# The first mixer's projections in another order: two heads' queries and keys first, the retention inputs late

## The chip, the core and the metric

The kernel runs on one core of a Trainium2 chip. The metric is device time in microseconds for one execution of the whole program, lower is better. TensorE (PE) multiplies matrices into PSUM banks; VectorE (DVE), ScalarE (ACT) and GpSimd (POOL) do the elementwise work; SyncE (SP) issues most of the loads.

## The reference

A batch of 512 tokens by 1024 features goes through two blocks of two layers each. The first block is the one that the change touches (twice, once for each layer):

```python
for l in range(2):
    h = rms_norm(x, norm_mix_pre[l])
    q_da, k_da, v_da, q_r, k_r, v_r, g_r, u_pool = split(h @ w_in[l])   # 512 512 512 128 128 256 256 256 wide
    o_da = diff_attention(q_da, k_da, v_da, ...)   # 4 heads, rotary on q and k, two causal softmaxes each,
                                                   # a0 - lam * a1, times v, rms norm over the head
    o_ret = retention(q_r, k_r, v_r, g_r, ...)     # 4 heads, chunks of 128 tokens with a carried state,
                                                   # group norm, times silu(g)
    o_pool = pool_mixer(u_pool, ...)               # causal means over 2, 4, 8, 16 tokens, minus u, times pool_w
    x = x + rms_norm(concatenate([o_da, o_ret, o_pool]) @ w_out[l], norm_mix_post[l])
    x = x + rms_norm(conv_mlp(rms_norm(x, norm_mlp_pre[l])), norm_mlp_post[l])
```

The second block (feed-forward, another mixer, feed-forward) is not touched.

## The kernel before

The program is a row of ten stages: mix1 and mlp1 for each of the two layers, then ffn1, mix2 and ffn2 twice. All of them share one stream of weights. A chunk is 128 x 1024 numbers; SP loads it (`wraw`, three buffers), ACT rounds it to `whi` (L63) and DVE forms the rest `wlo` (L64), into four pairs of buffers. A chunk's pair is given back by `release`, and the call that gives it back also emits the ACT and DVE instructions that split the chunk four places later. Every dense product is made of three matmuls (hi x hi, hi x lo, lo x hi), so one chunk is 24 matmuls of 512 columns.

There are two ways of multiplying. `fm` makes features by tokens: one chunk, one PSUM bank, and then an evacuation; `fm(..., halves=True)` takes four chunks with four banks and goes through them twice, first for tokens 0 to 255, then for 256 to 511, in 24 matmuls of 256 columns each. `tm` makes tokens by features: four banks at once, one for each tile t of 128 tokens, and its three matmuls for one k go t = 0, 1, 2, 3; with `tail=n` the last n chunks go tile by tile, so that the banks finish one after another.

PSUM has eight banks: four of tag a and four of tag b. In a mixer stage one tag is for the dense products, the other for attention, retention and pooling. These three are written as generators: `diff_attention` (scores, weigh, turn, values, norm, store for 16 pairs of head and tile), `retention` and `pooling`. After each dense triple `tick` adds 640 ns to a clock of credit and steps `bg` and `side` until the credit is used up; what a generator yields is its price. This sets where their instructions stand on every engine; each engine then goes through its own instructions strictly in order. Names in what follows: `psc` scores, `e` their exponentials, `pat` their transposes, `po` values, `on` the normed values, `pot` their transposes (the last step of a head); `pkt`, `prs`, `pst`, `pr`, `rc`, `rsq`, `rn`, `prt` are retention in its order; `pl` and `ppy` are pooling. `mix` holds the eight input tiles of the output product.

Before the change the mixer's order is: `vg` (the retention's values and gate; token-major, tail=4, each token's transposes `ph` just ahead of its products), `v`, q0, k0, qr, kr (the retention's queries and keys), q1, k1, q2, k2, q3, k3, u1, u0 (pooling), and then the output product, whose rows of `w_out` are stored in MIX_ORDER, so that retention and pooling tiles come in at k = 0, 1, 5, 6 and head 3 at k = 7. Queries and keys are evacuated by `rope` (L496): `sh` on DVE (L499), `raw` on DVE (L500), a product on POOL (L501) and a sum on POOL (L502); then, on a later tick, a split on ACT and DVE into `fmq0h` and `fmq0l`. A PSUM bank `pa` is free when `sh` and `raw` have read it. In `fm` without halves these two are emitted ahead of the release of the chunk, with halves behind it.

Of the kernel before, what the change touches and what calls it, by code (L numbers as in the profile page):

```python
# [18 lines left out]
L = 2  # L19
D = 1024  # L20
# [13 lines left out]
MIX_ORDER = (4, 5, 0, 1, 2, 6, 7, 3)  # L34
# [57 lines left out]
class Block:  # L92
# [185 lines left out]
    def tm(self, nk, width, rows, evac, tag, tail=0, opens=False):  # L278
# [24 lines left out]
        for t in range(NT):  # L303
            if opens:
                self.flush(max(self.opened, t))
# [81 lines left out]
    def begin(self, gain):  # L387
# [25 lines left out]
        def turn(t):  # L413
            self.to_h(t, rows.pop(t), "b")
            if t == 1:
                self.st.n_split, self.opened = n_split, 1
# [4 lines left out]
        self.opened = 0  # L421
        self.later(math.inf, 0, lambda: turn(0))
# [103 lines left out]
    def mix1(self, l, next_gain, final):  # L526
# [4 lines left out]
        load = nc.sync.dma_start  # L531
# [12 lines left out]
        load(cols, a["mix_cols"][l])  # L544
        pw = ph.tile([128, 2, 128], F32, name="pw")
        rope_q, rope_k = [], []

        def late_loads():
            load = nc.gpsimd.dma_start
            self.load_masks(3)  # L550
# [27 lines left out]
        def to_fm(name, mask, tab):  # L578
            def evac(ps):
                fm[name] = new_fm(name)  # L580
                self.rope(fm[name], ps, mask, *tab)
            return evac
# [16 lines left out]
        def to_u(c):  # L599
            def evac(ps):  # L600
                self.until(lambda: ("scored", 1) in mix)
# [4 lines left out]
        def to_tm(dst):  # L606
            def evac(t, ps):
                nc.scalar.activation(dst[:, t], ps, AF.Copy)
            return evac

        h_rows = lambda k, t: [x[:, k, t * 128:(t + 1) * 128] for x in self.H]
        free = {"q2": ("scored", 0), "k2": ("scored", 0), "q3": "ret", "k3": ("scored", 1)}
# [3 lines left out]
        def to_vg(t, ps):  # L616
            nc.scalar.activation(vg[:, t, :256], ps[:, :256], AF.Copy)
            nc.scalar.activation(vg[:, t, 256:], ps[:, 256:], AF.Silu)

        self.tm(KD, 512, h_rows, to_vg, dense, tail=4, opens=True)  # L620
        late_loads()
        lambdas()
        self.tm(KD, 512, h_rows, to_tm(v_da), dense, tail=1)
        self.fm([da("q0"), da("k0")])
        self.bg.work.append(self.diff_attention(fm, v_da, neglam, cols[:, 0:1], mix))
        self.fm([to_fm("qr", self.ROPE32, rope_q), to_fm("kr", self.ROPE32, rope_k)])
        self.side.work.append(self.retention(fm, vg, cols[:, 2:4], mix))
        self.fm([da("q1"), da("k1")])
        self.fm([da("q2"), da("k2")])
        self.fm([da("q3"), da("k3")])  # L630
        self.fm([to_u(1), to_u(0)])
        self.side.work.append(self.pooling(u, share, pw, cols[:, 4:6], mix))

        def rows(k, t):
            k = MIX_ORDER[k]
# [8 lines left out]
    def diff_attention(self, fm, v, neglam, gcol, mix):  # L644
# [79 lines left out]
        for i in range(len(units) + 5):  # L724
# [5 lines left out]
            if 1 <= i <= len(units):  # L730
                weigh(*units[i - 1])
                yield 850
            if 2 <= i < len(units) + 2:
                turn(*units[i - 2])
                yield 850
            if 3 <= i < len(units) + 3:
                values(*units[i - 3])
                yield 850
# [12 lines left out]
    def retention(self, fm, vg, gcols, mix):  # L751
# [5 lines left out]
        yield 4000  # L757
# [8 lines left out]
        for h in range(4):  # L766
# [8 lines left out]
            yield 1500  # L775
        state = []
# [14 lines left out]
        for j in range(2):  # L791
# [15 lines left out]
            nc.gpsimd.tensor_mul(s, x, x)  # L807
            nc.vector.reduce_sum(st[:, 2], s, axis=AX)
# [6 lines left out]
            if j == 1:  # L815
                mix["ret"] = True
            yield 2500
# [446 lines left out]
def arrange(inp):  # L1264
# [65 lines left out]
```

## Time and profile before

| | us |
|---|---|
| median of 3 runs | 3435.41 (3434.85 to 3436.55) |
| the profiled execution, its own time | 3436.64 |
| its span in the profile | 3434.9 |
| first mixer stage, until the first product of the MLP | 0 to 243.4 |
| second mixer stage, from its first product to that of the MLP | 613.9 to 843.4 |
| mean granted clock of PE | 0.992 |

The profiled execution's time is 1.7 us above its span; the prediction adds its changes to that time. The first mixer stage also holds the program's opening (the loads of x and the norm of the first rows).

### The profile page before, as it was taken

How to read it: one execution, taken by the hardware profiler on the slowest of the kernel's cores; microseconds unless marked ns; L12 is line 12 of the kernel's file. 1: busy time of each engine (PE TensorE's matmuls, PEld its weight loads, DVE VectorE, ACT ScalarE, POOL GpSimd, SP SyncE). 2: the span in 40 equal slices, each digit the busy share in tenths (PEclk: the TensorE clock that was granted, in tenths of full speed). 3: DMA queues.
4: the chain of work that ended last, by engine and by line, in shares of the span. 5: the costliest groups of instructions: out<-in, count | busy, mean ns of one | idle time of the engine just before them, and what ended most of it. 6: DMA issues, size and time to landing. Idle time of an engine off the chain costs nothing.

```text
span 3434.9 us, 39516 instructions
## 1 busy us (share of the span) xinstructions
PE 3352.0 (98%) x16080; PEld 2770.5 (81%) x16080; DVE 1542.0 (45%) x2013; ACT 1192.8 (35%) x1886; POOL 356.3 (10%) x412
## 2 busy tenths in 40 slices
PE   8999999999999999999999999999999999999999
PEld 6778888767888888888688888888888878888887
DVE  4665542466555243323564533324332457453332
ACT  4344432434443232223533332223222443432222
POOL 2421110242110000000220100000000022010000
PEclk9999999999999999999999999999999999999999
DMA  4122332312233222232112232322232212223232
GB/s 158 49 75 86 104 112 92 108 50 75 86 105 111 92 93 96 95 104 97 59 64 77 90 103 95 104 92 97 95 104 98 96 51 68 82 91 103 94 103 80
DMA packets 87190, 311.99 MB, mean 91 GB/s; under 512 B 10368, under 2 KB 11072, under 8 KB 87008
## 3 DMA queue, kind: packets, MB, share of 16 engines
q1 hardware_dynamic: 85536, 305.17, 26.6%
q0 software_dynamic: 1472, 4.30, 0.4%
q8 instruction: 127, 2.08, 0.2%
q14 instruction: 55, 0.45, 0.0%
HBM read 307.32 MB, written 2.10 MB: 90 GB/s over the span
## 4 chain that ended last, share of the span: by engine, by line
PE 87%; DVE 6%; ACT 3%; POOL 2%; issue 2%; DMA 1%; DVEq 0%; POOLq 0%; ACTq 0%; SPq 0%
PE pa L177 17%; PE pa L178 17%; PE pa L179 17%; PE pb L183 10%; PE pb L184 10%; PE pb L185 10%; DVE wlo L64 1%; PE pz L1121 1%; PE ph L220 1%; PE pos L1121 1%; DVE xn L210 1%; PE pst L986 1%; DVE sh L499 1%; ACT whi L63 0%; PE psc L662 0%
## 5 line engine op out<-in xcount | busy, mean ns | idle before, releaser
L64 DVE TENSOR_TENSOR wlo<-wraw,whi 128x1024 fp32r<-128x1024 f32 x556 | 710.5, 1279 | 1113.1 <-ACT whi L63 1112.0
L177 PE MATMUL pa<-h_hi,whi 128*128 128x512 f32 (+1 forms) x3072 | 1164.5, 379 | 2.0 <-ACT h_hi L162 2.0
L178 PE MATMUL pa<-h_lo,whi 128*128 128x512 f32 (+1 forms) x3072 | 1145.3, 373 | 2.7 <-DVE h_lo L163 2.7
L179 PE MATMUL pa<-h_hi,wlo 128*128 128x512 f32 (+1 forms) x3072 | 1144.5, 373 | 0.0
L63 ACT ACTIVATE whi<-wraw 128x1024 fp32r<-128x1024 f32 x556 | 585.2, 1053 | 635.7 <-PE pb L185 540.7
L177 PEld LDWEIGHTS pa<-h_hi,whi 128*128 128x128 f32 x3072 | 580.5, 189 | 107.6 <-issue 4.9
L179 PEld LDWEIGHTS pa<-h_hi,wlo 128*128 128x128 f32 x3072 | 580.1, 189 | 101.3
L178 PEld LDWEIGHTS pa<-h_lo,whi 128*128 128x128 f32 x3072 | 581.0, 189 | 99.3 <-DVE h_lo L163 4.3
L183 PE MATMUL pb<-whi,hid_hi 128*128 128x512 f32 x1056 | 411.8, 390 | 0.0
L184 PE MATMUL pb<-wlo,hid_hi 128*128 128x512 f32 x1056 | 410.9, 389 | 0.0
L185 PE MATMUL pb<-whi,hid_lo 128*128 128x512 f32 x1056 | 410.9, 389 | 0.0
L183 PEld LDWEIGHTS pb<-whi,hid_hi 128*128 128x128 f32 x1056 | 198.2, 188 | 41.2
L185 PEld LDWEIGHTS pb<-whi,hid_lo 128*128 128x128 f32 x1056 | 198.2, 188 | 41.1
L184 PEld LDWEIGHTS pb<-wlo,hid_hi 128*128 128x128 f32 x1056 | 198.2, 188 | 40.7
L438 ACT ACTIVATE hid_hi<-act 128x512 fp32r<-128x512 f32 x88 | 55.6, 632 | 383.9 <-DVE act L449 383.9
L201 POOL TENSOR_TENSOR rs<-ss 128x1 f32<-128x1 f32 x44 | 12.0, 273 | 1601.8 <-ACT sqs L191 1601.8
L449 DVE TENSOR_TENSOR act<-act,pa 128x512 f32<-128x512 f32 x88 | 60.5, 687 | 210.3 <-PE pa L179 210.3
L458 DVE SCALAR_TENSOR_TENSOR cv<-pa,cw,cv 128x511 f32<-128x511 f32 (+1 forms) x176 | 131.5, 747 | 15.9 <-ACT cv L456 12.8
L445 ACT ACTIVATE act<-pa 128x512 f32<-128x512 f32 x88 | 52.5, 597 | 246.6 <-PE pa L179 246.6
L183 PE MATMUL pb<-whi,h_hi 128*128 128x512 f32 x256 | 108.0, 422 | 11.4 <-DVE fmraw L500 6.7
L184 PE MATMUL pb<-wlo,h_hi 128*128 128x512 f32 x256 | 102.9, 402 | 1.2 <-DVE wlo L64 1.2
L185 PE MATMUL pb<-whi,h_lo 128*128 128x512 f32 x256 | 102.7, 401 | 0.0
(323 smaller groups left out, 2934.5 us busy)
## 6 DMA issues: line engine op xcount, KB each, us to landing
wraw<-w_ffn SPq DMA_DIRECT2D x264, 512.0 KB, 3.2
wraw<-w_mix SPq DMA_DIRECT2D x160, 512.0 KB, 3.3
wraw<-w_mlp SPq DMA_DIRECT2D x132, 512.0 KB, 3.3
X<-x SPq DMA_DIRECT2D x4, 512.0 KB, 7.6
gain<-norm_ffn SPq DMA_DIRECT2D x4, 512.0 KB, 5.3
out<-xn SPq DMA_DIRECT2D x8, 256.0 KB, 2.0
gain<-norm_mix_pre SPq DMA_DIRECT2D x2, 512.0 KB, 5.5
rope_da<-c_rope SPq DMA_DIRECT2D x2, 512.0 KB, 8.4
```

What stands on the lines that cost most here:

```text
L63: self.nc.scalar.activation(hi, t, AF.Copy)
L64: self.nc.vector.tensor_sub(lo, t, hi.bitcast(F32))
L177: mm(ps, w[0], h[0], start=first, stop=False)
L178: mm(ps, w[0], h[1], start=False, stop=False)
L179: mm(ps, w[1], h[0], start=False, stop=last)
L183: mm(ps, h[0], w[0], start=first, stop=False)
L184: mm(ps, h[0], w[1], start=False, stop=False)
L185: mm(ps, h[1], w[0], start=False, stop=last)
L438: nc.scalar.activation(hid[0][:, f], h, AF.Copy)
L449: nc.vector.tensor_mul(g, g, ps)
L458: nc.vector.scalar_tensor_tensor(c[:, s:], ps[:, :T - s], cw[:, j, i:i + 1], c[:, s:], op0=OP.mult, op1=OP.add)
L1121: mm = lambda out, lhsT, rhs, first: nc.tensor.matmul(out, lhsT, rhs, start=first, stop=True, skip_group_check=True)
```

## The change

The projections of the first mixer go in another order: q0, k0, q1, k1 in halves of the tokens; the small `lambdas` computation; `v` (tail=1); q2, k2; q3, k3; qr, kr; `vg` (tail=1, no longer first); u1, u0; then the output product in natural order (heads 0 to 3, retention, pooling). Attention's generator is now started ahead of `v`, and asks for `v` tile by tile before it multiplies values. Retention waits for `vg` before its states. Pooling is put behind attention in `bg` in place of behind retention in `side`. Some yields are longer. The loads of `rope_da`, `lams`, `mix_cols` and the masks go out on POOL's queue at the head of the stage; they were on SP's (the masks on POOL's, later).

```diff
         def to_vg(t, ps):
...
-        self.tm(KD, 512, h_rows, to_vg, dense, tail=4, opens=True)
+            mix["vg", t] = True
+
+        self.fm([da("q0"), da("k0"), da("q1"), da("k1")], halves=True)
+        self.bg.work.append(self.diff_attention(fm, v_da, neglam, cols[:, 0:1], mix))
         late_loads()
         lambdas()
-        self.tm(KD, 512, h_rows, to_tm(v_da), dense, tail=1)
-        self.fm([da("q0"), da("k0")])
-        self.bg.work.append(self.diff_attention(fm, v_da, neglam, cols[:, 0:1], mix))
+        self.tm(KD, 512, h_rows, to_v, dense, tail=1)
+        self.fm([da("q2"), da("k2")])
+        self.fm([da("q3"), da("k3")])
         self.fm([to_fm("qr", self.ROPE32, rope_q), to_fm("kr", self.ROPE32, rope_k)])
         self.side.work.append(self.retention(fm, vg, cols[:, 2:4], mix))
-        self.fm([da("q1"), da("k1")])
-        self.fm([da("q2"), da("k2")])
-        self.fm([da("q3"), da("k3")])
+        self.tm(KD, 512, h_rows, to_vg, dense, tail=1)
         self.fm([to_u(1), to_u(0)])
-        self.side.work.append(self.pooling(u, share, pw, cols[:, 4:6], mix))
+        self.bg.work.append(self.pooling(u, share, pw, cols[:, 4:6], mix))
...
-        load = nc.sync.dma_start
+        load = nc.gpsimd.dma_start
         rope_da = ph.tile([128, 2, T], F32, name="rope_da")
...
         load(cols, a["mix_cols"][l])
+        self.load_masks(3)
...
             if 1 <= i <= len(units):
                 weigh(*units[i - 1])
-                yield 850
+                yield 950
...
             if 3 <= i < len(units) + 3:
+                while ("v", units[i - 3][1]) not in mix:
+                    yield 300
                 values(*units[i - 3])
-                yield 850
+                yield 950
             if 4 <= i < len(units) + 4 and units[i - 4][1] == NT - 1:
                 h = units[i - 4][0]
+                yield 1900
                 normed[h] = norm(h)
...
-        yield 4000
+        yield 6000
         sg = vg[:, :, 256:]
...
+        while ("vg", NT - 1) not in mix:
+            yield 300
+        yield 1000
         state = []
...
-    order = [tiles_b(w[:, :, 1792:2304], 512), tiles_b(w[:, :, 1024:1536], 512)]
-    order += pair(0) + [fa[:, 12:14]] + pair(1) + pair(2) + pair(3) + [fa[:, 19:20], fa[:, 18:19]]
-    w_out = inp["w_out"].reshape(L, KD, 128, D)[:, MIX_ORDER].reshape(L, D, D)
+    order = pair(0) + pair(1) + [tiles_b(w[:, :, 1024:1536], 512)] + pair(2) + pair(3)
+    order += [fa[:, 12:14], tiles_b(w[:, :, 1792:2304], 512), fa[:, 19:20], fa[:, 18:19]]
+    w_out = inp["w_out"]
```

What this does to the order of instructions is shown at three places of the first mixer stage (numbers behind a name tell buffers apart).

DVE around the evacuation of the first queries and keys, before. Here q0 (`pa_528`) and k0 (`pa_565`) come behind `vg` and `v`, and `sh` and `raw` stand ahead of the `wlo` that their chunk's release emits:

```order
L64 TENSOR_TENSOR wlo_522<-wraw_432,whi_521 128x1024
L499 STREAM_SHUFFLE sh_554<-pa_528 128x512
L500 TENSOR_TENSOR raw_553<-pa_528,rope_da_125 128x512
L64 TENSOR_TENSOR wlo_560<-wraw_462,whi_559 128x1024
L163 TENSOR_TENSOR fmq0l_591<-raw_553,fmq0h_590 128x512
L499 STREAM_SHUFFLE sh_595<-pa_565 128x512
L500 TENSOR_TENSOR raw_594<-pa_565,rope_da_125 128x512
L64 TENSOR_TENSOR wlo_601<-wraw_492,whi_600 128x1024
L163 TENSOR_TENSOR fmk0l_632<-raw_594,fmk0h_631 128x512
L499 STREAM_SHUFFLE sh_636<-pa_606 128x512
L500 TENSOR_TENSOR fmqr_635<-pa_606,rope_rq0_380 128x512
```

The same evacuations after. They follow the second half of each chunk; each now stands behind a `wlo`, and all four banks `pa_194`, `pa_219`, `pa_270`, `pa_309` (q0, k0, q1, k1) are emptied one right after the other:

```order
L496 TENSOR_TENSOR raw_378<-pa_194,rope_da_125 128x512
L63 TENSOR_TENSOR wlo_409<-wraw_186,whi_408 128x1024
L495 STREAM_SHUFFLE sh_415<-pa_219 128x512
L496 TENSOR_TENSOR raw_414<-pa_219,rope_da_125 128x512
L162 TENSOR_TENSOR fmq0l_442<-raw_378,fmq0h_441 128x512
L63 TENSOR_TENSOR wlo_449<-wraw_192,whi_448 128x1024
L495 STREAM_SHUFFLE sh_455<-pa_270 128x512
L496 TENSOR_TENSOR raw_454<-pa_270,rope_da_125 128x512
L162 TENSOR_TENSOR fmk0l_482<-raw_414,fmk0h_481 128x512
L63 TENSOR_TENSOR wlo_489<-wraw_376,whi_488 128x1024
L495 STREAM_SHUFFLE sh_495<-pa_309 128x512
L496 TENSOR_TENSOR raw_494<-pa_309,rope_da_125 128x512
```

What moved: four evacuations in a row stand where there were two of them among token-major products; and `v`, whose four banks `pb` are those four `pa`, is the next product on PE.

PE in the first part of the output product, before. Head 2's `pot` and head 3's `pat` and `po` stand among its products, as does pooling's `ppy`:

```order
L701 MATMUL po<-v_da,at 128x128 x2
L854 MATMUL ppy<-pl,pw 128x512
L183 MATMUL pb<-whi,mix_hi 128x512
L184 MATMUL pb<-wlo,mix_hi 128x512
L185 MATMUL pb<-whi,mix_lo 128x512
L719 MATMUL pot<-ident,on 128x128 x4
L690 MATMUL pat<-ident,e 128x128 x4
L183 MATMUL pb<-whi,mix_hi 128x512
```

PE after, at the place where `vg` ends and u1 begins (`pa`). The transposes of the last head's values `pot` stand three matmuls behind `vg`'s last one, and the first retention state `pst` three behind that:

```order
L176 MATMUL pa<-h_hi,whi 128x512
L177 MATMUL pa<-h_lo,whi 128x512
L178 MATMUL pa<-h_hi,wlo 128x512
L713 MATMUL pot<-ident,on 128x128 x4
L176 MATMUL pa<-h_hi,whi 128x512
L177 MATMUL pa<-h_lo,whi 128x512
L178 MATMUL pa<-h_hi,wlo 128x512
L779 MATMUL pst<-vg,kt 128x256
```

What moved: the last head ends before the output product begins, and retention's states come behind `vg`, thus behind all of attention.

POOL from the last splits of queries and keys to the end of pooling, before. Retention's rows are further ahead, and pooling (`pl`) shares the stretch with attention's small `oms`:

```order
L501 TENSOR_TENSOR sh_1327<-sh_1327,rope_da_125 128x512
L502 TENSOR_TENSOR raw_1326<-raw_1326,sh_1327 128x512
L167 TENSOR_SCALAR oms_1226<-oms_1226 128x4
L168 TENSOR_TENSOR oms_1226<-oms_1226,mhalf_83 128x4
L843 TENSOR_TENSOR pl_1575<-fmu1_1433 128x511
L843 TENSOR_TENSOR pl_1586<-pl_1575 128x510
L843 TENSOR_TENSOR pl_1616<-pl_1586 128x508
L167 TENSOR_SCALAR oms_1454<-oms_1454 128x4
L168 TENSOR_TENSOR oms_1454<-oms_1454,mhalf_83 128x4
L843 TENSOR_TENSOR pl_1637<-pl_1616 64x504
L843 TENSOR_TENSOR pl_1685<-fmu0_1541 128x511
```

POOL after, from retention's second normalisation to the end of pooling:

```order
L814 TENSOR_TENSOR rn_1714<-rsq_1699,rst_1694 128x512
L807 TENSOR_TENSOR rsq_1741<-rc_1739 128x512
L842 TENSOR_TENSOR pl_1773<-fmu1_1672 128x511
L842 TENSOR_TENSOR pl_1779<-pl_1773 128x510
L166 TENSOR_SCALAR rst_1736<-rst_1736 128x8
L167 TENSOR_TENSOR rst_1736<-rst_1736,mhalf_83 128x8
L811 TENSOR_TENSOR rsq_1741<-rc_1739,vg_130 128x512
L814 TENSOR_TENSOR rn_1786<-rsq_1741,rst_1736 128x512
L842 TENSOR_TENSOR pl_1794<-pl_1779 128x508
L842 TENSOR_TENSOR pl_1803<-pl_1794 64x504
L842 TENSOR_TENSOR pl_1825<-fmu0_1746 128x511
L842 TENSOR_TENSOR pl_1834<-pl_1825 64x510
```

What moved: retention's second half and all of pooling stand next to each other, and the output product, which reads both, comes right behind.

## Rows read from the trace of the kernel before

**Rows 1.** Both stages: length, busy PE PEld DVE ACT POOL, then PEclk, DMA share, GB/s.

```profile
46.50:242.90 196.40, 184.22 (x930) 144.51 (x929) 115.51 (x227) 76.89 (x187) 61.75 (x62) 0.97 0.18 62
649.40:843.40 194.00, 181.45 (x931) 142.21 (x930) 115.88 (x228) 77.38 (x188) 61.75 (x62) 0.98 0.19 62
```

**Rows 2.** Waits of PE in the second mixer stage: total, times, longest.

```profile
PE pot L719 <- DVE on L713: 2.4, 1, 2.4
PE pr L795 <- ACT e L669: 2.4, 1, 2.4
PE pkt L762 <- POOL fmkr L502: 1.3, 1, 1.3
PE pb L183 <- ACT vg L618: 1.3, 1, 1.3
PE psc L657 <- ACT e L669: 1.0, 3, 0.4
```

**Rows 3.** Timeline of PE, first mixer stage: start, duration, instruction, [idle before].

```profile
11.84 0.80 PE L183 MATMUL pb<-whi,h_hi 128*128 128x512 f32 x1 [1.63 <-ACT whi L63]
15.40 1.91 PE L220 MATMUL ph<-ident,xn 128*128 128x128 f32 x8
...
44.39 0.50 PE L183 MATMUL pb<-whi,h_hi 128*128 128x512 f32 x1 [1.24 <-ACT vg L618]
```

**Rows 4.** Timeline of PE, second mixer stage.

```profile
620.03 1.38 PE L220 MATMUL ph<-ident,xn 128*128 128x128 f32 x8 [3.20 <-DVE xn L210]
621.16 0.48 PE L183 MATMUL pb<-whi,h_hi 128*128 128x512 f32 x1
...
624.82 0.47 PE L183 MATMUL pb<-whi,h_hi 128*128 128x512 f32 x1
...
647.21 0.50 PE L183 MATMUL pb<-whi,h_hi 128*128 128x512 f32 x1 [1.28 <-ACT vg L618]
```

**Rows 5.** Timeline of PE: full-width products five apart, half-width products seven apart.

```profile
46.80 0.39 PE L184 MATMUL pb<-wlo,h_hi 128*128 128x512 f32 x1
...
47.94 0.39 PE L183 MATMUL pb<-whi,h_hi 128*128 128x512 f32 x1
...
254.13 0.28 PE L177 MATMUL pa<-h_hi,whi 128*128 128x256 f32 x1
...
254.97 0.28 PE L178 MATMUL pa<-h_lo,whi 128*128 128x256 f32 x1
```

**Rows 6.** Timeline of ACT, DVE, POOL: a lone split, then the evacuation of q0.

```profile
65.89 1.23 DVE L64 TENSOR_TENSOR wlo<-wraw,whi 128x1024 fp32r<-128x1024 f32 x1 [4.51 <-ACT whi L63]
...
69.67 1.06 ACT L63 ACTIVATE whi<-wraw 128x1024 fp32r<-128x1024 f32 x1 [3.32 <-PE pa L178]
69.91 0.74 DVE L499 STREAM_SHUFFLE sh<-pa 128x512 f32<-128x512 f32 x1
70.55 0.67 DVE L500 TENSOR_TENSOR raw<-pa,rope_da 128x512 f32<-128x512 f32 x1
70.74 1.29 POOL L501 TENSOR_TENSOR sh<-sh,rope_da 128x512 f32<-128x512 f32 x1 [35.81 <-DVE sh L499]
71.14 1.97 DVE L64 TENSOR_TENSOR wlo<-wraw,whi 128x1024 fp32r<-128x1024 f32 x1
72.11 2.15 POOL L502 TENSOR_TENSOR raw<-raw,sh 128x512 f32<-128x512 f32 x1
...
74.29 0.63 ACT L162 ACTIVATE fmq0h<-raw 128x512 fp32r<-128x512 f32 x1 [3.56 <-POOL raw L502]
74.95 0.69 DVE L163 TENSOR_TENSOR fmq0l<-raw,fmq0h 128x512 fp32r<-128x512 f32 x1 [1.84 <-ACT fmq0h L162]
```

**Rows 7.** Groups of instructions, POOL and DVE, second mixer stage: busy, mean ns.

```profile
L843 POOL TENSOR_TENSOR pl<-pl 128x510 f32<-128x510 f32 (+3 forms) x4 | 4.4, 1092 | 9.5 <-DVE pl L842 6.4 <-DVE oms L711 3.0
L168 POOL TENSOR_TENSOR rst<-rst,mhalf 128x8 f32<-128x8 f32 x2 | 3.3, 1662 | 0.2
...
L713 DVE TENSOR_TENSOR on<-po,oms 128x512 f32<-128x512 f32 x4 | 2.8, 692 | 0.2
```

More of the change, by code (lines that the diff above doesn't have):

```diff
@@ L32 @@
 STAGES += [(kind, l) for l in range(L) for kind in ("ffn1", "mix2", "ffn2")]
-MIX_ORDER = (4, 5, 0, 1, 2, 6, 7, 3)
 N_CHUNKS = {"mix1": 20 + 8, "mlp1": 2 * KF + KF, "ffn1": 3 * KF, "ffn2": 3 * KF, "mix2": 40 + 4 + 8}
@@ L276, in fm_block, with tm @@
             self.tick(MM3 * n / 512)
-    def tm(self, nk, width, rows, evac, tag, tail=0, opens=False):
+    def tm(self, nk, width, rows, evac, tag, tail=0):
         per = CHUNK // width
@@ L303, in tm @@
         for t in range(NT):
-            if opens:
-                self.flush(max(self.opened, t))
             for c in range(n_chunks - head):
@@ L415, in turn @@
             if t == 1:
-                self.st.n_split, self.opened = n_split, 1
+                self.st.n_split = n_split
         chain(0)
@@ L420, in begin @@
         n_split, self.st.n_split = self.st.n_split, 2
-        self.opened = 0
-        self.later(math.inf, 0, lambda: turn(0))
+        self.later(0, 0, lambda: turn(0))
         self.later(200, 1, lambda: scaled(1))
@@ L548, in late_loads @@
         def late_loads():
-            load = nc.gpsimd.dma_start
-            self.load_masks(3)
             for src, tabs in (("c_rope_rq", rope_q), ("c_rope_rk", rope_k)):
@@ L579, in evac @@
             def evac(ps):
+                self.until(lambda: ("scored", 1) in mix)
                 fm[name] = new_fm(name)
@@ L600, in evac @@
             def evac(ps):
-                self.until(lambda: ("scored", 1) in mix)
+                self.until(lambda: ("scored", 2) in mix)
                 u[c] = new_fm(f"u{c}")
@@ L604, in to_u, with to_v @@
             return evac
[L606 to L609, printed above, removed]
+        def to_v(t, ps):
+            nc.scalar.activation(v_da[:, t], ps, AF.Copy)
+            mix["v", t] = True
         h_rows = lambda k, t: [x[:, k, t * 128:(t + 1) * 128] for x in self.H]
-        free = {"q2": ("scored", 0), "k2": ("scored", 0), "q3": "ret", "k3": ("scored", 1)}
+        free = {"k2": ("scored", 0), "q3": ("scored", 0), "k3": ("scored", 1)}
         da = lambda n: to_parts(n, free.get(n))
@@ L618, in to_vg @@
             nc.scalar.activation(vg[:, t, 256:], ps[:, 256:], AF.Silu)
-        self.tm(KD, 512, h_rows, to_vg, dense, tail=4, opens=True)
+            mix["vg", t] = True
+        self.fm([da("q0"), da("k0"), da("q1"), da("k1")], halves=True)
+        self.bg.work.append(self.diff_attention(fm, v_da, neglam, cols[:, 0:1], mix))
         late_loads()
         lambdas()
-        self.tm(KD, 512, h_rows, to_tm(v_da), dense, tail=1)
-        self.fm([da("q0"), da("k0")])
-        self.bg.work.append(self.diff_attention(fm, v_da, neglam, cols[:, 0:1], mix))
+        self.tm(KD, 512, h_rows, to_v, dense, tail=1)
+        self.fm([da("q2"), da("k2")])
+        self.fm([da("q3"), da("k3")])
         self.fm([to_fm("qr", self.ROPE32, rope_q), to_fm("kr", self.ROPE32, rope_k)])
         self.side.work.append(self.retention(fm, vg, cols[:, 2:4], mix))
-        self.fm([da("q1"), da("k1")])
-        self.fm([da("q2"), da("k2")])
-        self.fm([da("q3"), da("k3")])
+        self.tm(KD, 512, h_rows, to_vg, dense, tail=1)
         self.fm([to_u(1), to_u(0)])
-        self.side.work.append(self.pooling(u, share, pw, cols[:, 4:6], mix))
+        self.bg.work.append(self.pooling(u, share, pw, cols[:, 4:6], mix))
         def rows(k, t):
-            k = MIX_ORDER[k]
             self.until(lambda: k in mix)
@@ L731, in diff_attention @@
                 weigh(*units[i - 1])
-                yield 850
+                yield 950
             if 2 <= i < len(units) + 2:
                 turn(*units[i - 2])
-                yield 850
+                yield 950
             if 3 <= i < len(units) + 3:
+                while ("v", units[i - 3][1]) not in mix:
+                    yield 300
                 values(*units[i - 3])
-                yield 850
+                yield 950
             if 4 <= i < len(units) + 4 and units[i - 4][1] == NT - 1:
                 h = units[i - 4][0]
+                yield 1900
                 normed[h] = norm(h)
@@ L807, in retention @@
             nc.gpsimd.tensor_mul(s, x, x)
+            yield 1800
             nc.vector.reduce_sum(st[:, 2], s, axis=AX)
@@ L814, in retention @@
             xs.append(y)
-            if j == 1:
-                mix["ret"] = True
-            yield 2500
+            yield 1800
         yield 5000
```

## Prediction

> **What bounds the kernel now.** I read the waits of PE first, because PE is busy nearly all the time and only its gaps and its clock leave anything to win. In the mixer the named waits [rows 2] are single places: the last head's `pot` behind `on`, retention's `pr` behind attention's `e`, `pkt` behind the rope of `kr`, the first `v` products behind the evacuation of `vg`, and a few small `psc`. Next I read the windows, to get the loss of each mixer stage behind its opening. The first counted stretch [rows 1] is 196.40 us long with 184.22 busy, so 12.2 us idle; the granted clock is 0.97. Of PE's two levels, 1.2 and 2.4 GHz, the lower one then holds for about 6% of that time and costs half of it, 5.9 us. The second stretch is 194.00 with 181.45 busy (12.55 idle) at 0.98, which costs 3.9 us. Together 34.5 us can be won at most behind the openings, in both stages (two decimals of the clock leave about 1 us each way in each).
>
> Third, the openings by the timeline. In the first stage products begin at 11.84 on the first token tile alone, and the second tile is turned at 15.40 [rows 3]; in the second PE waits 3.20 us for the third tile's rows, then does nine products between 621.16 and 624.82 [rows 4]. A full-width product takes 1.14 us / 5 = 0.228 us, a half-width one 0.84 / 7 = 0.120 [rows 5]. Nine full ones would be 2.05 us, so the lower clock behind that wait cost 1.6 us. I use 1.6 for each stall of 2 us or more.
>
> **The change, part by part.**
>
> **Halves.** q0, k0, q1, k1 are 192 half-width products, 23.0 us, where `vg` was 96 full ones, 21.9: +1.1 us in each stage.
>
> **Opening.** `vg` began on one tile. The first half needs two, so in the first stage products start when the transposes of 15.40 are done, at 15.40 + 1.91 = 17.3. I add 1.8 for a clock that has to rise first (a little over the 1.6 above), 23.0 for the halves and 2.1 for two more groups of transposes (1.38 at the lower clock [rows 4], less at the higher): the four banks are full at 44.2. Before, the 96th product ended 1.24 us and nine products (the `v` products of tiles 0 to 2) ahead of 44.39, at 41.1. That is +3.1. In the second stage the third tile comes at 620.03 either way, with the same amount of dense work ahead of it, so only the 1.1 remains.
>
> **The values' banks.** `v` takes over the four banks of q0, k0, q1, k1, all filled at the end, 24 half products or 2.88 us apart, and each has to be read by `sh` and `raw`. In the order after, DVE has for each of them a `wlo`, `sh`, `raw` and a lower split: 1.97 + 0.74 + 0.67 + 0.69 = 4.07 us [rows 6], more than PE's 2.88. Let PE finish the halves at E. q0 ends at E-8.64; `whi` 1.06, a lone `wlo` 1.23, `sh` and `raw` free it by E-4.95, and POOL's product and sum (1.29, 2.15) run to E-2.15. k0 ends at E-5.76; its `wlo` lies beside POOL and takes 1.97; it is free at E-1.35. On ACT, `fmq0h` waits for POOL's sum and runs to E-1.5, with the `whi` of q1's release queued behind it, to E-0.45; then `wlo`, `sh`, `raw` give q1's bank back at E+2.9. POOL's sum for k0 ends at E+1.45, `fmk0h` at E+2.1, the last `whi` at E+3.15; `fmk0l`, `wlo`, `sh` and `raw` free k1's bank at E+7.0. PE does tiles 0 and 1 (six products, 1.37 us), waits 1.55 us for q1's bank, does three, waits 3.4 for k1's, does three: 4.95 us of stall where it was 1.24 and 1.28. So +3.6 in each stage. Behind PE's waiting products stand the first `psc`; nothing else is lost with them. I add 1.6 for the clock. Bounds: with every `wlo` at 1.23 us the stall is 3.5 and the clock may hold: +2.2; with every `wlo` stretched by a whole sum of POOL (1.23 + 2.15) it is about 9: +9.4 with the clock.
>
> The sum of the opening: 3.1 + 3.6 + 1.6 = 8.3 in the first stage, 1.1 + 3.6 + 1.6 = 6.3 in the second, **+14.6 us**.
>
> The row that decides this is a `wlo` of 1.97 us beside POOL against 1.23 alone [rows 6]: it grew by 0.74. The Trainium skill ("SBUF — State Buffer", section "Who interferes with whom") says that a VectorE instruction with two SBUF inputs contends with a GpSimd instruction that reads SBUF, and that the loser blocks fully and does not share. By that rule four evacuations in a row are a bad place for `wlo`, since POOL is hardly idle there; a whole sum would give the +9.4 above, some 4 us more in each stage than I take. The row shows less than a whole sum's 2.15, so I keep 1.97.
>
> **What goes.** Attention's rounds are spread over some 330 dense products in place of some 260, and retention no longer runs between them. So `pr` behind `e`, `pkt`, the wait for `vg` and most small `psc` waits go [rows 2], with their clock. I take all 34.5 us away and put back what the new order makes.
>
> **What comes.** (1) Last head: `on` stands behind the `wlo` that the release of `vg`'s last chunk emits. From that release: `whi` 1.06, an evacuation of `vg` ahead of it (0.6, as `fmq0h`), `wlo` 1.23, a small product (0.2) and `on` 0.69 [rows 6, 7], 3.8 us; PE is at `pot` after three products, 0.7: a wait of 3.1, and 1.6 of clock. It can't be much under the 2.4 of now, nor, with `wlo` at 1.97, over 4. (2) The end: retention's second half and pooling stand one behind the other on POOL. From the last `pr`: three DVE steps, 1.9 us (each as `sh` or `raw` or less); then on POOL `rsq` and two `pl`, the small step, the power 1.66, two products of 1.0 to 1.3, and two more `pl` of 1.09 [rows 7], 9.7 in all; 1.1 on DVE. That is 12.7 us, while PE has 45 products, 10.2 us, and 0.5 of transposes: 2.0 to 2.6 on the first `ppy`, and up to 0.9 on `prt` and the second. I take 3.0 and 1.6 of clock. What hides the rest is the output product; it would be 9 us more without that cover. (3) Retention's second `prs` waits for the exponentials of the last head, as `pr` did: 1.6, between nothing and the 2.4 of now. (4) Small waits (`po` three times, `pat`, the first scores), like the `psc` row [rows 2]: 2.8, between 1 and 4.
> Together 4.7 + 4.6 + 1.6 + 2.8 = 13.7 in each stage, **27.4 us**.
>
> **At nothing.** The loads on POOL's queue: in the second stage the four issues stand between rows of the norm where POOL waits for ACT anyway; `rope_da` is read 20 us later. Without that cover four issues would cost POOL some 4 us, each put at a `pl` of 1.09 [rows 7]. Natural order of `w_out` and the longer yields are only order, and counted in it.
>
> **Sum.** 14.6 - 34.5 + 27.4 = +7.5 us on the profiled execution's 3436.64, 3444.1. That execution stood 1.2 us over the median of the runs shown (3435.41), so the forecast for the median is **3443 us**.
>
> **The rivals.** A difference under 0.2%, 6.9 us, can hardly be told from none.
> - *Faster: the spreading pays in full.* Low contention of `wlo` (the opening costs 2 x 2.2 + 4.2 = 8.6), and only some 9 us of waits are left in the middle of each stage: 8.6 - 34.5 + 18 = -8, 3427 us. It decides if the middle's losses fall under 10 us a stage. For it: rows 2 hold only five waits over a microsecond, and all but `pot` lose their cause. Against it: DVE has as much to do as before.
> - *No change*: the opening as forecast, the middle at 10 to 12 us a stage: 14.6 - 34.5 + 22 = +2, 3437 us. For it: waits (2) and (3) rest on long sums of small rows, each of which can be off by a microsecond.
> - *Blocking*: `wlo` stretched by whole sums: 2 x 4.2 more, 3451 us.
> - *The middle regains little*: attention's chains of `e`, `at` and `on` wait wherever they stand, and 17 us a stage remain: 14.6 us slower, 3450 us.
> - *Loads*: `rope_da` late on POOL's queue, so that the first `sh` product waits; it would have to be 20 us late to be felt; then some 3445 us or more.
>
> **How the numbers follow.** My forecast (3440 to 3447) 0.33, of which 0.22 lies over the 0.2% bound; no change 0.25; faster 0.12; blocking 0.12; little regained 0.15; loads 0.03. Faster by over 0.2% 0.12, within it 0.11 + 0.25 = 0.36, slower 0.22 + 0.12 + 0.15 + 0.03 = 0.52. The range leaves out the faster case's lower part and the ends of blocking and of little regained together: 3430 to 3454.
>
> **What would show it.** In the changed profile: a wait of the first `v` products for DVE's `raw` in two pieces of about 1.5 and 3.4 us in each mixer stage, with the clock down behind it; the first product of the first stage at about 17; `pot` behind `on` about 3 us; `ppy` behind POOL's `pl` about 2.5; no `pr` behind `e`. I am wrong if `v` does not wait for `raw`, if the stretches behind the values' start still lose 16 us and more each, or if they lose under 10.

## The result, and the profile after

The changed kernel takes 3471.2 us (median; 3469.8 to 3472.36, 4 runs) beside 3435.98 for the kernel before on the same chips: ratio 1.01, 95% interval 1.0087 to 1.0113. It is slower by 35 us, 1%, where the forecast was 3443 with a range up to 3454. The page of the changed kernel:

```profile
span 3469.2 us, 39890 instructions
PE 3365.9 (97%) x16272; PEld 2789.2 (80%) x16272; DVE 1551.6 (45%) x2013; ACT 1192.0 (34%) x1885; POOL 356.1 (10%) x418
```

The span grew by 34.3 us, PE's busy time by only 14: PE stands still for longer. The windows behind the openings, from the sixth product of `v` to the first product of the MLP (columns as in [rows 1], which begins at the 19th, behind the wait for `vg`):

```profile
45.90:261.70 215.80, 192.98 (x945) 150.58 (x944) 119.32 (x230) 81.97 (x198) 58.10 (x66) 0.93 0.19 64
663.00:877.80 214.80, 192.40 (x938) 149.60 (x938) 117.77 (x228) 81.84 (x196) 58.10 (x66) 0.92 0.19 65
```

In the first stage 22.8 us are idle and the granted clock is 0.93, in the second 22.4 and 0.92. Before, it was 13.4 us with the 1.24 of the wait for `vg`, at 0.97, and 13.8 with its 1.28, at 0.98. So each stage stands still for about 9 us more, and more of it runs at the lower clock. What PE waited for in the first stage (total, times, longest), beside [rows 2]:

```profile
PE pb L182 <- DVE raw L496: 5.7, 2, 3.8
PE po L695 <- ACT e L663: 4.3, 2, 2.3
PE ppy L853 <- POOL pl L842: 3.1, 1, 3.1
PE pat L684 <- DVE on L707: 3.0, 1, 3.0
PE pot L713 <- DVE on L707: 2.5, 1, 2.5
PE prs L768 <- ACT e L663: 1.3, 1, 1.3
PE pat L684 <- ACT e L663: 1.1, 1, 1.1
PE prt L822 <- POOL rn L814: 0.9, 1, 0.9
```

All the waits that the forecast named are there (`v` for `raw`, `pot`, `ppy`, `prs`, `prt`), and `pr` behind `e` and `pkt` are gone. So is a wait that [rows 2] left out, `prt` behind `e`, 2.0 us. Two that it did not name head the middle: `po` behind `e` and `pat` behind `on`.

To set stages side by side I take, in each trace, the first stage up to the first half-width product of the MLP (243.39 us before, 261.72 after), and the second from the last product of the stage ahead of it to the same point. Differences to the kernel before, in us:

| kernel | stage 1 | stage 2 | whole, median |
|---|---|---|---|
| changed | +18.3 | +18.8 | 3471.2 |
| attention behind `v` (e1) | +6.2 | +6.9 | 3452.0 |
| e1, and `v` in other banks (e2) | -2.5 | -3.4 | 3432.8 |
| evacuation first (e3) | +18.6 | +17.1 | 3473.4 |
| opening of before (e4) | +7.8 | +10.5 | 3454.9 |
| rotary on VectorE (e5) | +18.7 | +15.2 | 3458.5 |
| yields of before (e6) | +6.2 | +4.1 | 3446.1 |
| loads on SP (e7) | +22.8 | +22.3 | 3482.6 |
| e2, pooling on VectorE (e8) | -4.0 | -5.1 | 3427.9 |
| e8 with yields of before (g1) | -2.6 | -3.9 | 3431.5 |
| before with the new yields (g2) | +3.8 | +4.5 | 3447.2 |
| attention's yields 850 (g3) | +4.7 | +8.4 | 3448.0 |
| no 1900 ahead of the norm (g4) | +13.0 | +8.8 | 3459.8 |
| no rotary sum, q2 to kr (h1) | +13.9 | +13.5 | 3465.9 |
| head 1 later by 6 (h2) | +17.9 | +15.7 | 3465.7 |
| head 1 later by 12 (h3) | +11.1 | +10.0 | 3459.6 |
| e8, second block's rotary on VectorE (i1) | -4.1 | -2.2 | 3416.0 |
| e8, both rotaries on VectorE (i2) | -3.2 | -4.2 | 3419.3 |

The medians of "before" beside them were 3435.35 to 3436.59. The rest of the program adds some 4 us at most of its own in either direction (more in e5, i1 and i2, which change the second mixer too), so the columns by stage say more than the whole time. They come from one execution each: e8 and i1, whose first block is the same program, differ by 2.9 us in stage 2. Single times of one kernel lie up to 10.5 us apart (g3: 3445.93 to 3456.41).

### The profile page after: what moved, and what is told of

Same layout as the page of the kernel before. It is cut to its first block, busy times and chain, and to the rows that moved or that the text cites. A ratio compares the mean times of both kernels' runs of the same rounds, so it can differ in the third digit from the quotient of the medians.

```text
span 3469.2 us, 39890 instructions
## 1 busy us (share of the span) xinstructions
PE 3365.9 (97%) x16272; PEld 2789.2 (80%) x16272; DVE 1551.6 (45%) x2013; ACT 1192.0 (34%) x1885; POOL 356.1 (10%) x418
## 4 chain that ended last, share of the span: by engine, by line
PE 69%; DVE 3%; ACT 2%; issue 1%; POOL 1%; DMA 0%; DVEq 0%; POOLq 0%; ACTq 0%
PE pa L176 14%; PE pa L177 14%; PE pa L178 14%; PE pb L182 8%; PE pb L183 8%; PE pb L184 8%; PE pz L1120 1%; DVE wlo L63 1%; PE ph L219 1%; PE pos L1120 1%; PE pst L985 0%; PE pod L985 0%; PE pm L1036 0%; POOL fmg L967 0%; DVE fmg L965 0%
## 5 line engine op out<-in xcount | busy, mean ns | idle before, releaser
L177 PE MATMUL pa<-h_lo,whi 128*128 128x512 f32 (+1 forms) x3136 | 1158.8, 370 | 3.4 <-DVE h_lo L162 3.4
L178 PE MATMUL pa<-h_hi,wlo 128*128 128x512 f32 (+1 forms) x3136 | 1157.7, 369 | 0.5 <-DVE wlo L63 0.5
L176 PEld LDWEIGHTS pa<-h_hi,whi 128*128 128x128 f32 x3136 | 595.3, 190 | 106.9 <-ACT h_hi L161 4.9
L178 PEld LDWEIGHTS pa<-h_hi,wlo 128*128 128x128 f32 x3136 | 594.8, 190 | 100.1 <-DVE wlo L63 0.8
L177 PEld LDWEIGHTS pa<-h_lo,whi 128*128 128x128 f32 x3136 | 595.5, 190 | 99.0 <-DVE h_lo L162 5.4
L200 POOL TENSOR_TENSOR rs<-ss 128x1 f32<-128x1 f32 x44 | 11.9, 271 | 1598.8 <-ACT sqs L190 1598.8
L182 PE MATMUL pb<-whi,h_hi 128*128 128x512 f32 x256 | 115.6, 452 | 17.7 <-DVE raw L496 11.0
```

The costliest lines, as they stand in the source:

```text
L176: mm(ps, w[0], h[0], start=first, stop=False)
L177: mm(ps, w[0], h[1], start=False, stop=False)
L178: mm(ps, w[1], h[0], start=False, stop=last)
L182: mm(ps, h[0], w[0], start=first, stop=False)
```

## The experiments

**The values' banks.** In e1 and e2 attention's generator starts behind `v`; e2 also gives `v` the four banks that attention does not use yet.

```diff
-        self.bg.work.append(self.diff_attention(...))
         late_loads()
         lambdas()
-        self.tm(KD, 512, h_rows, to_v, dense, tail=1)
+        self.tm(KD, 512, h_rows, to_v, self.bg_tag, tail=1)    # e2; in e1 still dense
+        self.bg.work.append(self.diff_attention(...))
```

> The changed kernel, with attention's generator started behind the values instead of ahead of them; nothing else. It is the control for the run with other banks. Theory A (the values' banks: PE stands still for the evacuation of q1 and k1, and the low clock behind it is the larger part of the loss): the wait of v for raw stays at 5.3 to 5.7 us a stage, the clock stays low behind it, and the time stays near the changed kernel's 3471 us (3465 to 3478). Theory B (attention's chains are late in the middle because VectorE's queue is, and how long attention is spread does not matter): po behind e and pat behind on are still there; also 3465 to 3478. Rival C (spreading attention earlier does pay): 5 to 10 us slower than 3471.

> As the run with attention started behind the values, but v is multiplied into the four PSUM banks of the other tag, so that it need not wait for the evacuations of q0, k0, q1, k1. Theory A: the wait of v for raw (5.3 to 5.7 us a stage) and the low clock behind it (some 4 to 5 us a stage) go: 18 to 22 us under the control run, near 3452. Theory B: only the wait itself goes, 8 to 11 us under the control, since the evacuations are as slow as before and meet attention's first rounds in their place.

e1 was a surprise: 3452 us (ratio 1.0047, 1.003 to 1.0064), 19 us under the changed kernel, with the wait of `v` still 5.4 us. None of the theories had that. The gain lies behind the stall. From there to the MLP (columns as in [rows 1]), the changed kernel and then e1:

```profile
62.00:261.70 199.70, 182.59 (x905) 144.02 (x904) 105.72 (x199) 77.28 (x185) 48.45 (x54) 0.95 0.17 59
60.00:249.60 189.60, 177.13 (x923) 139.29 (x922) 107.53 (x212) 77.89 (x193) 48.73 (x54) 0.99 0.18 63
```

Idle time fell from 17.1 to 12.5 us, and the granted clock rose from 0.95 to 0.99; counted as in the prediction (what it lacks of 1, times the length) that is 10.0 us of loss in the changed kernel and 1.9 in e1. The clock is the larger part of the gain. e2 took 3432.8 (0.9991, 0.9982 to 1.0), 19.2 less again: the wait is gone from the list, and so is the clock behind it, as theory A said. In e1's timeline of PE (start, duration, instruction, idle before) the price of the wait is seen by itself:

```profile
48.58 0.47 PE L182 MATMUL pb<-whi,h_hi 128*128 128x512 f32 x1 [1.90 <-DVE raw L496]
...
49.23 0.63 PE L184 MATMUL pb<-whi,h_lo 128*128 128x512 f32 x1
53.33 0.76 PE L182 MATMUL pb<-whi,h_hi 128*128 128x512 f32 x1 [3.47 <-DVE raw L496]
53.89 0.63 PE L183 MATMUL pb<-wlo,h_hi 128*128 128x512 f32 x1
...
58.59 0.63 PE L182 MATMUL pb<-whi,h_hi 128*128 128x512 f32 x1
59.01 0.49 PE L183 MATMUL pb<-wlo,h_hi 128*128 128x512 f32 x1
59.34 0.39 PE L184 MATMUL pb<-whi,h_lo 128*128 128x512 f32 x1
```

Two waits, 1.90 and 3.47 us, and between them three products. Neighbours are 0.43 us apart from 53.89 until 59.01, which is the lower clock (granted clock 0.50 from 48.98 to 59.22). From 48.58 to 59.34 there are 17 products, 3.9 us at full clock, and 3.47 of waiting; the other 3.4 us are clock.

**The order inside the evacuation** (e3).

```diff
                         if h == 1:
-                            self.st.release(i)
                             got[j][2](ps)
+                            self.st.release(i)
```

> The changed kernel, but where queries and keys are made in halves each bank is read out before its chunk is given back, so that sh and raw stand ahead of the wlo of the split. (The MLP stages use the same routine.) Theory A: q1's bank comes back about 2 us earlier, k1's about 2 us earlier, so the wait of v falls from 5.3 to 5.7 us to 1 to 3 us, and the time by 5 to 15 us, to 3456 to 3466. Rival (VectorE has more work in four evacuations than PE in four half chunks, so the order of it matters little): the wait stays above 4 us and the time within 4 us of 3471.

3473.4 us (1.0106, 1.0091 to 1.0121), within the rival's 4 us of 3471, with 3.9 us of the wait left, a hair under the rival's 4. The first of the two waits is gone, but the second and the clock behind it (granted 0.50 from 52.1 to 62.1) are as long as in the changed kernel. So the order alone gains nothing; the rival's account, that VectorE has more to do than PE, fits.

**The old opening** (e4): `vg` and `v` first, then all queries and keys, not in halves, `qr`, `kr`, `u`, and the rest as changed. Attention's generator then starts behind k0.

> The opening of the kernel before (vg on one tile, then v) with the rest of the changed kernel: q0 k0 q1 k1 q2 k2 q3 k3 in a row, not in halves, then qr kr, u1 u0, the output product in natural order, pooling behind attention, the longer yields, the loads on POOL's queue. If the opening is all of the loss (theory A): the time of the kernel before, 3436 within 5 us, or less. If the middle is half of it (theory B: late evacuations in attention's rounds, and retention and pooling at the end): 3448 to 3458, with po behind e, pat behind on and ppy behind pl still in the list of waits.

3454.9 us (1.0056, 1.0041 to 1.0071), in theory B's band: the opening is not all of it. Of the waits that theory B named, `po` and `ppy` are there and `pat` behind `on` is not. The longest of e4 behind the opening:

```profile
PE pot L717 <- DVE on L711: 3.3, 1, 3.3
...
PE ppy L857 <- DVE pl L852: 2.8, 1, 2.8
PE po L699 <- ACT e L667: 2.6, 1, 2.6
```

**Pace and place of the rounds.** e6 takes back all yields; g3 only attention's three (950 to 850); g4 only the 1900; g2 puts the new yields into the kernel before; h2 and h3 delay head 1's four rounds alone, by six and by twelve dense products.

```diff
-                yield 950
+                yield 850                  # e6, g3; three places
...
-                yield 1900                 # e6, g4: left out
...
+            if i == NT:
+                yield 1280                 # h2; 2560 in h3
```

> The changed kernel with the yields of the kernel before (850 in attention, none ahead of the norm, 4000 ahead of retention, none and 2500 in its normalisation). Attention's rounds then fall elsewhere against the evacuations of q2, k2, q3, k3, qr, kr. Theory P (the loss of the middle hangs on where rounds and evacuations meet): the list of waits changes, and the middle moves by 5 us or more in either direction (3455 to 3466, or 3476 to 3485). Rival (the middle's loss comes from the order itself): within 4 us of 3471, with the same waits.

> The changed kernel with attention's three yields at 850 in place of 950; the 1900 ahead of the norm and retention's yields as changed. A round of attention then takes 12 dense products, half a chunk, in place of 13 or 14, so that every round lies alike against the evacuations, which come every 24. Theory P with the pace of the rounds as cause: most of the 25 us of the pace run, 3446 to 3456. If retention's yields or the 1900 were the cause: 3465 or more.

> The changed kernel without the 1900 ahead of the norm; all else as changed. It shifts the heads behind the first by about nine products and leaves the pace of the rounds. If the pace is the cause: within 6 us of 3471. If the place of the norm is: 3455 to 3463, with the wait of pat behind on (3.0 us) gone.

> The kernel before with the changed kernel's yields (950 in attention, 1900 ahead of the norm, 6000 ahead of retention, 1800 and 1800 in its normalisation), nothing else. Rival Y: 10 to 25 us slower, 3446 to 3460. Theory P: the rounds move by a few products and the waits of pr, prt, pot change places, in either direction by up to 10 us, 3426 to 3446.

> The changed kernel with one more yield ahead of head 1's scores: its four rounds move behind by six dense products (a quarter of a chunk), the other heads stay where they are. Theory P (what counts is where a round lies against an evacuation): the wait of po behind e at head 1 changes by a microsecond or more, with the clock behind it; the time moves by 3 to 8 us, up or down. Rival (how early attention stands is what costs): within 2 us.

> The same with twelve products, half a chunk. Theory P: another time again, 3 to 8 us from 3471 or from the run with six; with the last round of head 1 now well behind q2's evacuation, I expect the first wait of po gone and 3461 to 3468. Rival: within 2 us of 3471.

e6 took 3446.1 us (1.0042, 1.0028 to 1.0056): 25 us off, more than either band of theory P, with no dense product moved. g3 alone took 3448.0, as expected if the pace of the rounds is the cause. But g4, which leaves the pace, took 3459.8, without the wait of `pat` behind `on`, as expected if the place of the norm is. h2 took 3465.7 (`po` 3.0 us, where it was 4.3) and h3 3459.6, 1 us under my band (`po` 3.0, and `pat` behind `on` gone too); both are outside the rival's 2 us. So pace alone isn't the cause. The gains don't add up either: g3's 23 us and g4's 11 would be more than the 25 of e6, which has both edits. What the runs share is that some rounds lie elsewhere against the evacuations. In g3 a round takes 12 products, half a chunk, and all rounds of a head lie alike; of the middle's waits these are left there:

```profile
PE ppy L853 <- POOL pl L842: 3.1, 1, 3.1
PE prs L768 <- ACT e L663: 1.3, 1, 1.3
PE pat L684 <- DVE mix_lo L746: 1.0, 2, 0.6
PE pot L713 <- DVE on L707: 0.9, 1, 0.9
PE prt L822 <- POOL rn L814: 0.9, 1, 0.9
```

`po` went from 4.3 us to 0.6 and `pat` behind `on` is gone. g2 took 3447.2, 11 us more than before. That is rival Y's band, 1 us outside theory P's, but its waits are those of theory P: `po` behind `e`, 0.6 us before, heads its first stage.

```profile
PE po L701 <- ACT e L669: 7.1, 2, 4.0
```

**Both cures together** (g1): e8's kernel (below) with e6's yields.

> The kernel with v in the other banks, attention behind the values and pooling's sums on VectorE (3427.9 us), now also with the yields of the kernel before. Theory P (the longer yields put attention's rounds where they meet the evacuations; starting attention behind v had moved the rounds already, so both cures take away the same loss): within 6 us of 3428. Rival Y (the longer yields cost by themselves, whatever the rounds meet): the 25 us of the pace run come off here too, 3400 to 3408.

3431.5 us (0.9985, 0.9976 to 0.9995), 3.6 more than without them, where the two intervals overlap. The 25 us do not come off a second time: starting attention behind `v` and the shorter yields take away the same loss. Theory P holds here, and rival Y falls.

**Why rounds are late there** (e5, h1). The changed kernel's timeline ahead of the first wait of `po`:

```profile
95.34 1.28 DVE L659 TENSOR_REDUCE st<-psc 128x1 f32<-128x512 f32 x2
...
96.65 1.26 POOL L498 TENSOR_TENSOR raw<-raw,sh 128x512 f32<-128x512 f32 x1
96.66 1.28 DVE L660 TENSOR_SCALAR st<-st 128x2 f32<-128x2 f32 x1
...
98.03 0.69 ACT L663 ACTIVATE e<-psc,st 128x512 f32<-128x512 f32 x1 [3.86 <-DVE rec L673]
...
98.86 0.67 PE L695 MATMUL po<-v_da,at 128*128 128x128 f32 x2 [2.00 <-ACT e L663]
```

DVE's scale of 128 x 2 numbers (L660) takes 1.28 us. It starts with GpSimd's rotary sum (96.65, 1.26 us) and ends with it. The exponentials, the copy behind them on ACT and PE's `po` all wait for that. e5 moves the rotary's product and sum to VectorE; h1 leaves the sum out for q2 to kr.

```diff
-        nc.gpsimd.tensor_mul(sh, sh, sin)
-        nc.gpsimd.tensor_add(out, out, sh)
+        nc.vector.tensor_mul(sh, sh, sin)      # e5
+        nc.vector.tensor_add(out, out, sh)     # e5; in h1 the sum is left out, the product stays on gpsimd
```

> The changed kernel with the rotary's product and sum on VectorE in place of GpSimd, so that no large GpSimd instruction lies beside VectorE in the mixer's first part. Theory C (what makes attention late in the middle is that GpSimd's rope sum holds up small VectorE instructions: the 128x2 scale took 1.28 us in place of 0.17 just ahead of each wait of po): no such stretched instruction any more, the waits of po (4.3 us) and of pat behind on (3.0) fall to half or less, 5 to 12 us gained in all, 3459 to 3466. Rival Q (VectorE's queue is simply too long there): the evacuations get 1.4 us longer on VectorE, so the waits of po, pat and v for raw grow, and the time goes to 3475 or more.

> The changed kernel, leaving out the rotary's sum on GpSimd (1.3 to 2.2 us each) for q2, k2, q3, k3, qr and kr, so that their rotary is incomplete; q0, k0, q1, k1 are as before, and every instruction of PE stands where it stood. Theory C (attention's rounds are late where GpSimd's sum holds a small VectorE instruction): the stretched 128x2 and 128x4 instructions (1.2 to 1.3 us) are gone, po behind e falls from 4.3 us to 2 or less and pat behind on from 3.0 to 2 or less, 8 to 20 us gained, 3451 to 3463. Rival Q (VectorE's own queue of wlo, sh, raw is what they wait for): the waits stay within 0.5 us each and the time within 4 us of 3471.

h1 took 3465.9 us, and its mixer stages gained 4.4 and 5.3 us, between theory C's forecast and rival Q's. `po` behind `e` fell from 4.3 to 2.1 us and `pat` behind `on` from 3.0 to 1.9, about as theory C said. The same instructions in h1:

```profile
94.85 1.28 DVE L660 TENSOR_REDUCE st<-psc 128x1 f32<-128x512 f32 x2
...
96.17 0.17 DVE L661 TENSOR_SCALAR st<-st 128x2 f32<-128x2 f32 x1
...
96.43 0.69 ACT L664 ACTIVATE e<-psc,st 128x512 f32<-128x512 f32 x1 [2.75 <-DVE rec L674]
...
97.26 0.49 PE L696 MATMUL po<-v_da,at 128*128 128x128 f32 x2 [0.89 <-ACT e L664]
```

The scale takes 0.17 us, and `po` comes with 0.89 us of idle time in place of 2.00. So the hold-up is real, and worth some 5 us a stage; it is not all of the 12 that the rounds' place costs (e1). In e5 the hold-up is gone too, but VectorE does the work itself, and the waits are nearly as long:

```profile
PE po L695 <- ACT e L663: 3.9, 2, 2.9
PE pat L684 <- DVE on L707: 2.5, 1, 2.5
```

e5 took 3458.5 us, at the edge of theory C's band, but not for its reason: the first block's mixer stages hold 3.2 of the 12.7 us, the rest lies behind them. Neither theory C nor rival Q is the whole. GpSimd's part is shown by h1; that VectorE's own queue holds the rounds up as well is how I read e5. The rest of the 12 us was not separated further.

**The loads** (e7): back on SP's queue, the masks later.

> The changed kernel with the loads of rope_da, lams, mix_cols on SP's queue and the masks later, as in the kernel before. If the loads cost nothing (as forecast): 3468 to 3474 us and the same waits. If they cost: 3466 or less, and other waits at the openings of the two mixer stages.

One run, 3482.6 us: 11 more, not within my band; 8 of them lie in the two mixer stages. Loads and masks moved together here. The granted clock is 0.50 from 49 to 66 us, 17 us where it was 10, and only the masks show among the waits: attention now starts so early that masks issued late hold it up:

```profile
PE psc L652 <- DMA masks<-c_bf: 2.8, 1, 2.8
```

**The end of the stage** (e8).

```diff
-                nc.gpsimd.tensor_add(y[p, n:], x[p, n:], x[p, :T - n])
+                nc.vector.tensor_add(y[p, n:], x[p, n:], x[p, :T - n])
```

> The kernel with v in the other banks (3432.8 us) with the sums of pooling on VectorE in place of GpSimd. It takes away half of the long GpSimd chain at the end of the stage. If the end costs what I reckoned (about 4 us of waits for ppy and prt in each stage, and 1.6 us or more of low clock behind them): ppy no longer waits, and the time falls by 8 to 14 us, to 3419 to 3425. Rival (the output product's inputs come late anyway, by retention): prt takes the wait over, and the time falls by under 4 us.

3427.9 us (0.9974, 0.9964 to 0.9983), 4.9 less, between the 8 of my forecast and the rival's 4. `ppy` (3.1 us in e2) no longer waits, but `prt` does, as the rival said:

```profile
PE pat L684 <- DVE on L707: 3.2, 2, 1.6
PE prt L822 <- POOL rn L814: 2.8, 1, 2.8
```

**The best version** (i1: e8 with the second block's rotary on VectorE; i2: both blocks').

> The best kernel so far (v in the other banks, attention behind v, pooling's sums on VectorE; 3427.9 us), with the rotary's product and sum of the second block's mixer on VectorE. In the run with all rotaries on VectorE the mixer stages of the first block gained only 3 us together and the rest of the 12.6 us came from stages behind them. If that gain belongs to the second mixer: 5 to 10 us less, 3418 to 3423. If it was the scatter of those stages: within 4 us of 3428.

> The same with the rotary of both mixers on VectorE. Theory C (GpSimd's sums hold up VectorE's small instructions in attention's rounds): the stretched 128x4 instruction (1.22 us) ahead of each of the two waits of pat behind on (1.6 us each) is gone, those waits fall under 1 us, and the first block's mixer stages gain 2 to 5 us each over the run with the second mixer alone. Rival Q (VectorE's queue): the waits grow or stay, and the first block's mixer stages gain nothing or lose.

i1 took 3416.0 us (0.9942, 0.9926 to 0.9959), the fastest of all, 11.9 under e8 where I had expected 5 to 10. That gain belongs to the second mixer, which the change does not touch. i2 took 3419.3 (0.9952, 0.9937 to 0.9967), not clear of i1, and the first block's mixer stages did not gain the 2 to 5 us each of theory C (1.0 us more in the first, 2.0 less in the second). In i2 `pat` behind `on` fell from 3.2 to 2.1 us, toward what theory C said, and `po` (1.1 in e8) and another `pat` (1.5) rose by as much together:

```profile
PE prt L822 <- POOL rn L814: 2.8, 1, 2.8
PE pat L684 <- DVE on L707: 2.1, 2, 1.1
PE pat L684 <- DVE mix_lo L746: 2.0, 1, 2.0
PE po L695 <- ACT e L663: 1.7, 1, 1.7
```

## Why the prediction was wrong

Its sum was +14.6 - 34.5 + 27.4 = +7.5 us for the two mixer stages; they measured +37.1. Two terms were too small: the waits of attention's rounds in the middle, some 24 us, and the stall of the values' banks, some 6.

**Halves, opening: right.** The first product came at 16.69 us (forecast 17.3) and the four banks were full at 44.8 (44.2). The first product of `v` came 3.9 us later in the first stage (forecast 3.1) and 1.1 in the second (1.1). e2 is the changed kernel without the bank stall, with attention at another place. For it my terms give 14.6 less 2 x (4.95 + 1.6) for the stall, and 7.1 less for the middle: -5.6. Its stages measured -5.9. That is in part luck: `pot` waits 1.0 us there and not 3.1, `po` and `pat` 5.8 and not 2.8.

**The values' banks: right mechanism, a term too small.** The waits were 1.90 and 3.81 us (forecast 1.55 and 3.4); the timeline shows the DVE chain that I had added up:

```profile
44.19 1.62 POOL L498 TENSOR_TENSOR raw<-raw,sh 128x512 f32<-128x512 f32 x1
...
44.59 2.31 DVE L63 TENSOR_TENSOR wlo<-wraw,whi 128x1024 fp32r<-128x1024 f32 x1
...
47.45 0.67 DVE L496 TENSOR_TENSOR raw<-pa,rope_da 128x512 f32<-128x512 f32 x1
...
48.26 0.47 PE L182 MATMUL pb<-whi,h_hi 128*128 128x512 f32 x1 [1.90 <-DVE raw L496]
...
48.98 1.59 POOL L498 TENSOR_TENSOR raw<-raw,sh 128x512 f32<-128x512 f32 x1
...
49.37 2.28 DVE L63 TENSOR_TENSOR wlo<-wraw,whi 128x1024 fp32r<-128x1024 f32 x1
...
52.20 0.67 DVE L496 TENSOR_TENSOR raw<-pa,rope_da 128x512 f32<-128x512 f32 x1
...
53.01 0.76 PE L182 MATMUL pb<-whi,h_hi 128*128 128x512 f32 x1 [3.81 <-DVE raw L496]
...
53.57 0.63 PE L183 MATMUL pb<-wlo,h_hi 128*128 128x512 f32 x1
```

What failed was the step "I use 1.6 for each stall of 2 us or more". The stall cost 19.2 us in both stages (e1 to e2), 9.6 a stage, where I had 6.55. Of the difference the clock is the larger part: 3.4 us in e1's first stage, where I had 1.6. The 1.6 came from one wait of 3.20 us ahead of steady products; in e1 a second, longer wait came while the clock was still low.

I also misread the row that I had weighed. `wlo` grew to 1.97 us [rows 6], less than a whole sum, and I took that against full blocking. But the instruction beside it was the product, 70.74 to 72.03; `wlo` started at 71.14 and ended at 73.11, 1.1 us behind the product's end: as if it had waited for that end, 0.89 us, and run then. Above, `wlo` starts 0.4 us behind the start of GpSimd's sum, 44.19 to 45.81, and ends at 46.9, again 1.1 us behind its end. By the Trainium skill ("SBUF — State Buffer", section "Who interferes with whom"), the ports that VectorE shares with GpSimd are an exclusive lock: the instruction that comes first holds them and the other blocks fully, not by a share. These rows agree, and so does the scale that ends with the sum. The rival "blocking" was still wrong in its price: `wlo` began 0.4 us behind the instruction beside it in all three rows and so lost 0.9 to 1.2 us, not a whole sum.

**What goes, what comes: the step that failed.** "I take all 34.5 us away and put back what the new order makes" rested on a hand-made list of new waits. `pot` (2.5, forecast 3.1), `ppy` and `prt` (4.0, forecast 3.0) and `prs` (1.3, forecast 1.6) were about right. The 2.8 us of "small waits" were `po` 4.3, `pat` behind `on` 3.0 and `pat` behind `e` 1.1: 8.4, and I had given them no low clock. Behind the two waits of `po` and that of `pat` behind `on` the granted clock fell to 0.50 (from 99.0, 133.2 and 143.4 us on). Behind the stall the first stage lost 10.0 us to the clock, where I had 3.2. These two, 5.6 and 6.8 us, make up about the 12 a stage. I had priced where instructions stand on PE and not what lies beside them on VectorE and GpSimd at that moment: `e`, `on` and the rotary's evacuations meet there. e1, e6 and h3 show it: with rounds at another place the same work costs 12, 13 and 8 us less a stage. By e1 that is some 24 us of the 29.6 that I missed; the stall is the rest. GpSimd's hold-up took some 10 of them in h1; how much of the rest is VectorE's own queue stays open.

**The longer yields "are only order, and counted in it": wrong.** With attention started ahead of `v`, they were the difference between rounds that lie clear of the evacuations and rounds that lie on them, 25 us by e6. With attention behind `v` they cost nothing (g1).

**The loads, put at nothing: not so with the masks.** Loads and early masks together save some 8 us in the mixer stages (e7, one run, one profile); which of it is the loads' is not separated.

Of the rivals, "the middle regains little" came nearest, but its 17 us a stage was still too low. In the first stage 22.8 us idle and 15.1 of clock (0.07 of 215.80), less the stall's 9.6, leave 28. The prediction's own sign of being wrong, 16 us and more a stage, came true.

## What to carry to other kernels

When work is moved between fixed chunks, lay the new round against what the other engines do in that same stretch: two chains that share an in-order queue, or run on two engines that hold each other up, cost by where they meet, and a change of pace can cost more than a change of order. Before a product takes over banks, count whether the engine that empties them is faster than the one that fills them; if not, give it other banks (19 us here). And price a stall with the clock that follows: look whether a second wait comes before the clock is back.

## What the runs showed of the hardware that was not expected

- A VectorE scale of 128 x 2 numbers took 1.28 us beside a GpSimd sum of 1.26 us, and 0.17 us without it.
- GpSimd is held up as well: the rotary's sum took 2.15 us beside `wlo` [rows 6], and 1.26 us ahead of `po`, where only the small scale lay beside it.
- After waits of 1.90 and 3.47 us (e1), PE's products stayed 0.43 us apart, the lower clock, for more than 5 us of steady work, and 3.4 us were lost in all.
- A wait of 2.0 us in the middle (`po`, at 98.86) was followed by a granted clock of 0.50; e1's waits in attention's rounds, 1.6 us at most, were not.
